# A decoder layer on one Trainium2 core: the gate product in rounded parts, and the last 32 columns of the projection in four column groups

## The chip, the cores and the metric

The kernel runs on one core of a Trainium2 chip. The metric is the device time of one execution in microseconds. Engines are named as in the profile: PE is TensorE's matmul, PEld its weight load, DVE is VectorE, ACT is ScalarE, POOL is GpSimd, and SP is SyncE, which here issues most of the DMAs. Each engine works through its own instructions strictly in the order in which the program gives them to it; an instruction that waits holds up all that stand behind it on the same engine.

## What is computed

One decoder layer on x of (1, 256, 1024) float32. Cut to what matters here:

```
z = rms_norm(x, norm1_g) @ w_in                 # 1024 -> 1824 (RWKV) + 1536 (MoBA) + 2048 (gates)
z[:, :1824] is mixed with its row before: z + mu * (shift_right(z) - z)
r, k, v = three blocks of 512 columns           # columns 0 .. 1535
xw, xa, xg = z[..., 1536:1600], z[..., 1600:1664], z[..., 1664:1824]   # 64, 64 and 160 columns
decay = exp(-exp(w_log)),  w_log from decay_bias + tanh(xw) @ w_decay_up
a = sigmoid(aaa_bias + xa @ w_aaa_up)
g = sigmoid(xg) @ w_gate_up                     # 160 -> 512: "the gate product"
y = delta-rule recurrence over 256 steps, 8 heads of 64, then a group norm
rwkv = (y + bonus(r, k, v)) * g
moba = softmax attention of 8 heads on q, k, v of the MoBA columns
out = x + merge(rwkv, moba) @ w_out, then a gated MLP with a causal convolution (1024 -> 2 x 2816 -> 1024)
```

## The kernel before

**Weights in two parts.** Nearly all of the PE's work is products of the large weight matrices with 256 tokens. A float32 weight tile of 128x1024 numbers (512 KB) comes from memory through SP's queue (`load_next`, L241), in the order of one list, `queue` (L329 ff.). ACT rounds it to fp32r into `whi` (L253, `split_hi`), DVE subtracts that from the original into `wlo` (L263, `split_lo`), and the PE forms three products: `whi` with the input's high part, `whi` with its low part, `wlo` with its high part. In the functions `wst` (L291, L293, L296) the weight is stationary, and 24 matmuls of 128x256 use up one tile; in `xst` (L312, L313, L316) the input is stationary and the weights stream by. Few buffers stand between these steps (4 for raw tiles, 4 further ones for the first loads, 4 of `whi`, 3 of `wlo`, 3 PSUM banks under the name `acc`), so that each engine runs only a tile or two ahead of the PE.

**Small products in float32.** The two low-rank products of decay and a (L549), the gate product (L787, L788), the sums over heads (L585, L786) and the recurrence use float32 matmuls directly, which the trace records as two matmul passes each.

**The first steps.** Transposes of the normalised input, the first two weight tiles (columns 1536 to 1791: xw, xa and the first 128 columns of xg) and the filler matmuls of `keep_warm` (L374: five matmuls of 128x512 on a tile of ones, between the transposes of the two token halves) are written in a fixed order for all engines. `shift` (L354 on ACT, L355 on DVE) mixes a projected block with its row before. The remaining 32 columns of xg are made from a third weight tile, the tail: columns 1696 to 1823, 128 of them, of which 96 are there already. Its loads are pieces of 512 bytes, its 24 matmuls are the ones of `run(wst(p, 1, hh, hl))`, and its result goes to `xg[:, 1]`. The weight rows that would count a column twice are zero in `wgu[:, 1]`.

**What sets the order after that.** Two threads written as Python generators, "chain" (L543 ff., the RWKV recurrence) and "bulk" (L1122 ff., projections k, r, MoBA's q, v, and so on), are interleaved by a small planner (L1152 ff.). A thread yields a cost (the PE time that it has just issued) and a latency (how long until it can go on), and the planner picks the next thread by these estimates. The order on PE follows from it; a scheduler then sets the order on ACT, DVE, POOL and SP from its own model of the program.

**The chain** around the change: the products of decay and a (`at`, `ch`, L549), eight sigmoids on ACT (`sg`, `av`, L554), a scan over tokens on DVE (L561), then exponentials on ACT. The mixed k is squared on ACT (`sq`, L579) and summed over heads on PE (`pss`, L585). Later the chunk matrices `G` are made (L660), moved by DMA through a scratch `d` into `Tb` (L670, L672), inverted on DVE (`tmp`, `mid`, `Xb`, L697 to L728), moved through `d` again into `X` (L740), and used by the PE in 64 matmuls of 32x32, `pp` (L814). Between the `G` and the `pp` of the PE's order stand weight products of bulk and the block `bon`: bonus sums (L786) and gate product (L787, L788) in two halves of 12 passes, with a yield of 2.7 after each half.

In the diff `b2`, `b4`, `b8`, `t1`, `by` and `cst.tile` hand out buffers of different pools, `atp()`, `chp()` and `acc()` hand out PSUM banks.

Of the kernel before, what the change touches and what calls it, by code (L numbers as in the profile page):

```python
# [9 lines left out]
F32 = mybir.dt.float32  # L10
# [8 lines left out]
S = 256  # L19
# [3 lines left out]
CW = 512  # L23
# [13 lines left out]
def body(tc, x, positions, norm1_g, w_in, rwkv_mu, w_decay_up, decay_bias, w_aaa_up,  # L37
# [5 lines left out]
    with ctx:  # L43
# [59 lines left out]
        ones = cst.tile([128, 512], mybir.dt.bfloat16, name="ones")  # L103
# [10 lines left out]
        rst = cst.tile([128, 4 * S], mybir.dt.bfloat16, name="rst")  # L114

        def late_consts():
            pool.memset(rst, 1.0)
            pool.memset(rst.rearrange("p (c i) -> p c i", i=64)[:, :, 0:1], 0.0)
            pool.memset(wgu[0:96, 1], 0.0)
# [39 lines left out]
        wgu = cst.tile([128, 2, CW], F32, name="wgu")  # L159
# [4 lines left out]
        for r, n in ((mu1[0:1792].rearrange("(n c) -> n c", c=128), 14),  # L164
                     (mu1[1696:1824].rearrange("(n c) -> n c", c=128), 1),
# [4 lines left out]
        loads += [(wdu[0:64], w_decay_up[0]), (wdu[64:128], w_aaa_up[0]),  # L170

                  (wgu[:, 0], w_gate_up[0, 0:128]), (wgu[96:128, 1], w_gate_up[0, 128:160])]
# [156 lines left out]
        queue += kh(win, 1536, 256) + kh(win, 1696, 128)  # L329
# [27 lines left out]

        def first_steps():
# [23 lines left out]
            nc.gpsimd.dma_start(*loads.pop(4))  # L382
# [8 lines left out]
            for t in range(2):  # L391
# [23 lines left out]
                if t == 0:  # L415
                    keep_warm(5)
# [55 lines left out]
            late_consts()  # L472
            xwa = t1("xwa")
            xg = b2("xg", [128, 2, S])
            shift(xwa, p[:, 0:256], 12)
            act.activation(xwa[0:64], xwa[0:64], AF.Tanh)
            shift(xg[:, 0], p[:, 256:512], 13)
            split_lo()
            split_hi()
            return xwa, xg  # L480

        E = mybir.EngineType
        with tc.manual_schedule(engines={E.PE, E.Activation, E.DVE, E.Pool}):
            xwa, xg = first_steps()
# [14 lines left out]
        p = acc()  # L499
        run(wst(p, 1, hh, hl))  # L500
        shift(xg[:, 1], p[:, 0:256], 14)
# [41 lines left out]
        def chain():  # L543

            sg, av, kp = b4("sg"), b4("av"), b4("kp")
            pw = [[(chp if j else atp)() for _ in range(2)] for j in range(2)]
            for ct in range(4):
                for n, lo_ in enumerate((0, 64)):
                    pe.matmul(pw[ct // 2][n][:, ct % 2 * 256:ct % 2 * 256 + 256],  # L549
                              wdu[lo_:lo_ + 64, ct * 128:(ct + 1) * 128],  # L550
                              xwa[lo_:lo_ + 64], start=True, stop=True)
            for ct in range(4):
# [3 lines left out]
            yield 2.2, 3.0  # L556
            act.activation(xg[:, 0], xg[:, 0], AF.Sigmoid)
            act.activation(xg[:, 1], xg[:, 1], AF.Sigmoid)
# [221 lines left out]
            A1 = b4("A1")  # L780
            for j in range(2):
                p, pg = (chp(), chp("pg")) if j else (atp(), atp("pg"))
                for i in range(2):
# [3 lines left out]
                    pe.matmul(pg[:, os], wgu[:, 0, cs], xg[:, 0], start=True, stop=False)  # L787
# [563 lines left out]
```

## Time and profile before

| | before |
|---|---|
| median of 3 runs | 412.95 us (411.76 to 413.96) |
| the profiled execution's own time | 411.65 us |
| its span in the trace | 409.5 us |
| PE busy | 402.8 us, 98% of the span |
| ACT, DVE busy | 234.1 us (57%), 317.9 us (78%) |
| POOL busy | 35.1 us (9%) |
| memory read | 68.76 MB, 171 GB/s over the span |

The span is the stretch from the first to the last instruction of the profiled execution; 2.15 us of its time lie around it. Matmuls overlap one another in the pipeline, so what one costs is read from the distance between two starts and not from its duration.

### The profile page before, as it was taken

Reading aid. Unit: us, or ns where it says so; the run is one execution under the profiler, and the core shown is the slowest. Engines: PE = TensorE matmul, PEld = TensorE weight load, DVE = VectorE, ACT = ScalarE, POOL = GpSimd, SP = SyncE. Lnnn points to the kernel's source line nnn. Section 1 sums busy time; section 2 is a strip of 40 time slices with the busy share of each in tenths; the row PEclk is TensorE's granted clock in tenths of the full one; section 3 lists DMA queues with packets and bytes.
Section 4 is the critical chain, followed back from the end, with each engine's and each line's share of the span. In section 5 each row is a group of like instructions: output and inputs, shape, how many; then the busy total and the mean of one; then the engine's idle time right before and its main releaser. Section 6 shows DMA issues by size and latency. Waiting matters only on the chain.

```text
span 409.5 us, 8251 instructions
## 1 busy us (share of the span) xinstructions
PE 402.8 (98%) x3266; PEld 352.6 (86%) x3266; DVE 317.9 (78%) x535; ACT 234.1 (57%) x393; POOL 35.1 (9%) x67
## 2 busy tenths in 40 slices
PE   8999999999999999999999999999999999999996
PEld 4999898898899889999988888888888888888885
DVE  3878999769547886677975898968769678697694
ACT  6999576254567774443554864635545555465450
POOL 8600410123100010000000000000000000000000
PEclk9999999999999999999999999999999999999999
DMA  8964556642953153366565557566655656656612
GB/s 256 317 216 120 172 174 173 196 125 72 232 163 106 53 154 106 107 205 205 189 204 175 156 158 228 179 205 186 210 176 173 209 185 199 202 168 203 196 54 102
DMA packets 60042, 70.72 MB, mean 173 GB/s; under 512 B 6530, under 2 KB 50325, under 8 KB 60005
## 3 DMA queue, kind: packets, MB, share of 16 engines
q1 hardware_dynamic: 59078, 69.79, 56.9%
q0 software_dynamic: 880, 0.41, 0.6%
q8 instruction: 25, 0.41, 0.4%
q14 instruction: 13, 0.10, 0.1%
q10 hardware_dynamic: 46, 0.01, 0.0%
HBM read 68.76 MB, written 1.44 MB: 171 GB/s over the span
## 4 chain that ended last, share of the span: by engine, by line
PE 85%; DVE 8%; DMA 3%; issue 1%; ACT 1%; POOL 1%; POOLq 0%; DVEq 0%; ACTq 0%
PE acc L1232 20%; PE acc L1237 10%; PE acc L291 7%; PE acc L293 7%; PE acc L296 7%; PE f L1252 4%; PE f L1254 4%; PE f L1256 4%; PE acc L312 4%; PE acc L313 3%; PE acc L316 3%; DVE wlo L263 2%; PE idle L452 1%; PE idle L374 1%; DMA X<-d 1%
## 5 line engine op out<-in xcount | busy, mean ns | idle before, releaser
L253 ACT CAST whi<-raw 128x1024 fp32r<-128x1024 f32 x123 | 128.7, 1051 | 106.7 <-PE acc L1232 41.0
L263 DVE TENSOR_TENSOR wlo<-raw,whi 128x1024 fp32r<-128x1024 f32 x123 | 150.7, 1229 | 42.8 <-PE acc L1237 14.0
L1232 PE MATMUL acc<-hx,whi 128*128 128x512 f32 x352 | 89.5, 395 | 0.0
L1232 PEld LDWEIGHTS acc<-hx,whi 128*128 128x128 f32 x352 | 63.4, 188 | 12.4
L291 PE MATMUL acc<-hx,whi 128*128 128x256 f32 x232 | 58.9, 289 | 0.6 <-DVE qkv L989 0.6
L293 PE MATMUL acc<-hx,whi 128*128 128x256 f32 x232 | 56.7, 280 | 0.0
L1237 PEld LDWEIGHTS acc<-hx,wlo 128*128 128x128 f32 x352 | 46.8, 188 | 4.0
L1237 PE MATMUL acc<-hx,wlo 128*128 128x256 f32 x352 | 47.4, 277 | 0.0
L291 PEld LDWEIGHTS acc<-hx,whi 128*128 128x128 f32 x232 | 43.8, 189 | 2.8 <-issue 2.1
L293 PEld LDWEIGHTS acc<-hx,whi 128*128 128x128 f32 x232 | 43.8, 189 | 0.1
L296 PE MATMUL acc<-hx,wlo 128*128 128x256 f32 x232 | 36.2, 279 | 0.0
L1254 PE MATMUL f<-whi,hb 128*128 128x512 f32 x80 | 31.2, 390 | 0.0
L1256 PE MATMUL f<-wlo,hb 128*128 128x512 f32 x80 | 31.2, 390 | 0.0
L1252 PE MATMUL f<-whi,hb 128*128 128x512 f32 x80 | 31.2, 389 | 0.0
L296 PEld LDWEIGHTS acc<-hx,wlo 128*128 128x128 f32 x232 | 31.0, 189 | 0.0
L1242 DVE TENSOR_REDUCE an<-acc 128x256 f32<-128x512 f32 x22 | 14.2, 686 | 9.4 <-PE acc L1237 9.4
L312 PE MATMUL acc<-whi,hx 128*128 128x512 f32 x48 | 19.8, 413 | 0.0
L313 PE MATMUL acc<-whi,hx 128*128 128x512 f32 x48 | 18.8, 393 | 0.0
L1256 PEld LDWEIGHTS f<-wlo,hb 128*128 128x128 f32 x80 | 15.0, 188 | 3.2
L1252 PEld LDWEIGHTS f<-whi,hb 128*128 128x128 f32 x80 | 15.0, 188 | 2.8
L1254 PEld LDWEIGHTS f<-whi,hb 128*128 128x128 f32 x80 | 15.0, 188 | 2.8
L316 PE MATMUL acc<-wlo,hx 128*128 128x512 f32 x48 | 14.9, 392 | 0.0
(319 smaller groups left out, 616.5 us busy)
## 6 DMA issues: line engine op xcount, KB each, us to landing
raw<-in_w_ffn_up_dram SPq DMA_DIRECT2D x44, 512.0 KB, 4.1
raw<-in_w_in_dram SPq DMA_DIRECT2D x42, 512.0 KB, 4.7
raw<-in_w_ffn_down_dram SPq DMA_DIRECT2D x22, 512.0 KB, 4.1
raw<-in_w_out_dram SPq DMA_DIRECT2D x8, 512.0 KB, 4.3
x<-in_x_dram SPq DMA_DIRECT2D x8, 256.0 KB, 3.4
raw<-in_w_branch_b_dram SPq DMA_DIRECT2D x4, 512.0 KB, 3.4
raw<-in_w_branch_a_dram SPq DMA_DIRECT2D x4, 512.0 KB, 4.6
out_dram<-o SPq DMA_DIRECT2D x3, 256.0 KB, 2.1
```

The costliest lines, as they stand in the source:

```text
L253: act.copy(hi[:, :k * c], raw[:, :k * c])
L263: eng.tensor_tensor(lo[:, :n], raw[:, :n], hi[:, :n].bitcast(F32), op=OP.subtract)
L291: pe.matmul(om, wh[:, k, ms], xh[:, k0 + k], start=k0 + k + m == 0, stop=False, skip_group_check=True)
L293: pe.matmul(om, wh[:, k, ms], xl[:, k0 + k], start=False, stop=False, skip_group_check=True)
L296: pe.matmul(om, wl[:, k, ms], xh[:, k0 + k], start=False, stop=k0 + k == nk - 1 and m == n - 1, skip_group_check=True)
L312: pe.matmul(ps_[t], xh[:, K, ts], wh[:, k], start=K == 0, stop=False)
L313: pe.matmul(ps_[t], xl[:, K, ts], wh[:, k], start=False, stop=False)
L1232: pe.matmul(ps_[m], wh[:, k, m * 128:m * 128 + 128], hx[:, k0 + k].rearrange("p a s -> p (a s)"), start=k0 + k == 0, stop=False, skip_grou ...
L1237: pe.matmul(ps_[m][:, 0:S], wl[:, k, m * 128:m * 128 + 128], hh[:, k0 + k], start=False, stop=k0 + k == 7, skip_group_check=True)
L1252: pe.matmul(fin[f], hb[:, 0, i, ts], wh[:, 0, cs], start=st, stop=False, skip_group_check=f == 3)
L1254: pe.matmul(fin[f], hb[:, 1, i, ts], wh[:, 0, cs], start=False, stop=False, skip_group_check=f == 3)
L1256: pe.matmul(fin[f], hb[:, 0, i, ts], wl[:, 0, cs], start=False, stop=False, skip_group_check=f == 3)
```

## The change

1. The tail tile, its 24 matmuls, its split into parts and its shift go. A tile `wtr` of 8x32 columns (128 KB, in pieces of 128 bytes) is loaded by SP third, behind the second raw tile. Sixteen float32 matmuls with 32 columns each (L488 of the changed file) go into four groups of 32 PSUM partitions, group g taking the k-blocks g and g + 4. DVE copies the result (`tls`), and one float32 matmul with a constant `fold3` (L584) adds the four groups and repeats the sum three times over 96 partitions, where it is shifted into `xgt` (L589, L590). POOL makes `fold3` with four small copies.
2. The gate product's inputs and weights are split into fp32r parts: `wgh` and `wgl`, `xgp` in two parts, and on 96 partitions `wgt` and `xtp`, which hold all three products of the 32 columns. `gate_parts` makes them with four casts on ACT and four subtractions on DVE; its weights `wgr` are loaded by SP behind the projection of k. The eight float32 matmuls become sixteen fp32r matmuls of 256 columns.
3. Both halves of `bon` are issued in one run, with one yield of 2.8.
4. `keep_warm(5)` becomes `keep_warm(3)`.
5. The second PSUM bank of MoBA's query product comes from `chp` instead of `acc`.
6. The first stage of `pp` and `P` is 16 columns wide instead of 32.
7. Yields: the chain begins with 0, 1.0, and its first cost is 2.6; in the group norm the latencies before the transposes `pc` are 7.0, 5.5, 5.5 and 0.8 for the four chunks, where they were 5.5, 5.5, 5.5 and 2.8. The attention's query and key pieces wait for the chain's turn (`joined`).
8. `ones` and `rst` live in other buffers, and the row of mu for the 32 columns is loaded four times.

The diff, cut to its core:

```diff
-        queue += kh(win, 1536, 256) + kh(win, 1696, 128)
+        queue += kh(win, 1536, 256)
...
                 load_next(i == 0, early=i >= NRAW)
+                if i == 1:
+                    nc.sync.dma_start(wtr, win[:, :, 1792:1824])
...
-                    keep_warm(5)
+                    keep_warm(3)
...
+            tl = chp("tl")[:, 0:S]
+            for n, xx in enumerate((hh, hl)):
+                for k in range(8):
+                    g = k % 4
+                    pe.matmul(tl[32 * g:32 * g + 32], wtr[:, k], xx[:, k].bitcast(F32), start=n == 0 and k < 4,
+                              stop=n == 1 and k >= 4, skip_group_check=True)
...
+            dve.tensor_copy(tls, tl)
...
-        p = acc()
-        run(wst(p, 1, hh, hl))
-        shift(xg[:, 1], p[:, 0:256], 14)
...
+        def gate_parts():
+
+            for w, o in wgr:
+                act.copy(o, w)
+            dve.tensor_tensor(wgl, wgr[0][0], wgh.bitcast(F32), op=OP.subtract)
+            dve.tensor_tensor(wgt[64:96], wgr[1][0][64:96], wgt[64:96].bitcast(F32), op=OP.subtract)
+            act.copy(xgp[:, 0], xg)
+            act.copy(xtp[0:96], xgt[0:96])
+            dve.tensor_tensor(xgp[:, 1], xg, xgp[:, 0].bitcast(F32), op=OP.subtract)
+            dve.tensor_tensor(xtp[32:64], xgt[32:64], xtp[32:64].bitcast(F32), op=OP.subtract)
...
+            yield 0, 1.0
...
+            pf = chp("fold")[0:96, 0:S]
+            pe.matmul(pf, fold3, tls, start=True, stop=True)
...
+            act.activation(xgt[0:96], pf, AF.Copy, scale=omm[0:96, 14:15])
+            dve.scalar_tensor_tensor(xgt[0:96, 1:S], pf[:, 0:S - 1], par[0:96, MU + 14:MU + 15], xgt[0:96, 1:S],
+                                     op0=OP.mult, op1=OP.add)
-            yield 2.2, 3.0
+            yield 2.6, 3.0
...
-                    pe.matmul(pg[:, os], wgu[:, 0, cs], xg[:, 0], start=True, stop=False)
-                    pe.matmul(pg[:, os], wgu[:, 1, cs], xg[:, 1], start=False, stop=True)
-                yield 2.7, 0.2
+                    pe.matmul(pg[:, os], wgh[:, cs], xgp[:, 0], start=True, stop=False)
+                    pe.matmul(pg[:, os], wgh[:, cs], xgp[:, 1], start=False, stop=False)
+                    pe.matmul(pg[:, os], wgl[:, cs], xgp[:, 0], start=False, stop=False)
+                    pe.matmul(pg[:, os], wgt[:, cs], xtp[0:96], start=False, stop=True)
+            yield 2.8, 0.2
...
-            pp = two_banks("pp", 32)
+            pp = two_banks("pp", 16)
...
-                    yield 0, 5.5 if c < 3 else 2.8
+                    yield 0, (7.0, 5.5, 5.5, 0.8)[c]
...
             yield from proj4("k", 4)
-            for _ in range(4):
+            wgr.append((b2("wgr", [128, CW]), wgh))
+            wgr.append((b2("wgr", [96, CW]), wgt))
+            nc.sync.dma_start(wgr[0][0], w_gate_up[0, 0:128])
+            for r in range(3):
+                nc.sync.dma_start(wgr[1][0][32 * r:32 * r + 32], w_gate_up[0, 128:160])
+            for _ in range(2):
                 nc.sync.dma_start(*loads.pop(0))
...
-                ps_ = [acc(), acc()]
+                ps_ = [acc(), acc() if i else chp("acc")]
...
             yield from attention_input(0)
+            gate_parts()
```

The line numbers of the changed file are some 7 to 40 higher than those of before. The order of instructions moves at three places.

On ACT, in the first steps, before: the casts of the tiles k1, k2 and k3 (the second to fourth tile of the projection of k), and the eight sigmoids.

```order
L253 CAST whi<-raw 128x1024 [waits DMAHW6_49,Pool_49]
L253 CAST whi<-raw 128x1024 [waits DMAHW7_49,Pool_49]
L354 ACTIVATE xg<-acc,omm 128x256 [waits PE_49]
L253 CAST whi<-raw 128x1024 [waits DMAHW0_49]
L554 ACTIVATE sg<-at,par 128x256 [waits PE_49]
L554 ACTIVATE av<-at,par 128x256 [waits PE_49]
```

The same place on ACT after the change; the two casts are k2 and k3.

```order
L260 CAST whi<-raw 128x1024 [waits DMAHW7_49,Pool_49]
L260 CAST whi<-raw 128x1024 [waits DMAHW0_49,Pool_49]
L593 ACTIVATE xg<-xg 128x256 [waits DVE_49]
L525 CAST wgh<-wgr 128x512 [waits DMAHW5_49]
L587 ACTIVATE sg<-at,par 128x256 [waits PE_49]
L587 ACTIVATE av<-at,par 128x256 [waits PE_49]
```

The cast of the gate's weights, although `gate_parts` stands late in the code, is ordered ahead of the eight sigmoids; it waits for the load of `wgr`, which SP issues behind the last tile of the projection of r.

On DVE, before: the low part of k2, the scan behind the sigmoids, and the low parts of k3 and r0. The rows left out are small operations of the rotary tables.

```order
L263 TENSOR_TENSOR wlo<-raw,whi 128x1024 [waits DMAHW7_49,DVE_49,PE_49]
...
L561 SCALAR_TENSOR_TENSOR L<-rst,sg 128x1024 [waits Activation_49,Pool_49]
L205 TENSOR_SCALAR turns<-turns 128x32 [waits DVE_49]
L211 SCALAR_TENSOR_TENSOR ang<-turns,ang 128x32 [waits DVE_49] x3
L263 TENSOR_TENSOR wlo<-raw,whi 128x1024 [waits DMAHW0_49,PE_49]
```

And after:

```order
L270 TENSOR_TENSOR wlo<-raw,whi 128x1024 [waits DMAHW7_49,Activation_49,Pool_49]
L526 TENSOR_TENSOR wgl<-wgr,wgh 128x512 [waits DMAHW5_49,Activation_49]
L597 SCALAR_TENSOR_TENSOR L<-rst,sg 128x1024 [waits Activation_49,Pool_49]
L590 SCALAR_TENSOR_TENSOR xgt<-fold,par,xgt 96x255 [waits Activation_49]
L270 TENSOR_TENSOR wlo<-raw,whi 128x1024 [waits DMAHW0_49,DVE_49,PE_49]
```

The subtraction of the gate's weights now stands between the low parts of k2 and k3, and the low part of k3 still stands behind the scan.

On PE, around `bon`, before: the second half of `bon` with a run of six projection matmuls ahead of it (one of six such runs between the first half and `pp`).

```order
L788 MATMUL pg<-xg,wgu 128x256
L312 MATMUL acc<-whi,hx 128x512
L313 MATMUL acc<-whi,hx 128x512
L312 MATMUL acc<-whi,hx 128x512
L313 MATMUL acc<-whi,hx 128x512
L316 MATMUL acc<-wlo,hx 128x512 x2
L786 MATMUL ch<-zr,bones 128x256
L787 MATMUL pg<-xg,wgu 128x256
L788 MATMUL pg<-xg,wgu 128x256
```

And after, the join of the two halves:

```order
L827 MATMUL pg<-xtp,wgt 128x256
L823 MATMUL ch<-zr,bones 128x256
L824 MATMUL pg<-xgp,wgh 128x256
L825 MATMUL pg<-xgp,wgh 128x256
L826 MATMUL pg<-xgp,wgl 128x256
L827 MATMUL pg<-xtp,wgt 128x256
```

The run of six is gone from between the halves. Five runs of six stand between `bon` and `pp` in both, so that 36 projection matmuls between the first half and `pp` have become 30; one run of six has moved behind the second half of `pp`. The rows of the chain from `G` to `X` on DVE, POOL and SP stand in the same order in both.

More of the change, by code (lines that the diff above doesn't have):

```diff
@@ L102, in body @@
         AR = b8("AR", [128, 16, 2, 64])
-        ones = cst.tile([128, 512], mybir.dt.bfloat16, name="ones")
+        ones = b2("ones", [128, 512], mybir.dt.bfloat16)
         jp = t1("jp", (128, 128), I32)
@@ L113, in body @@
         spread16 = cst.tile([128, 128], F32, name="spread16")
-        rst = cst.tile([128, 4 * S], mybir.dt.bfloat16, name="rst")
+        rst = b2("rst", [128, 4 * S], mybir.dt.bfloat16)
+        fold3 = cst.tile([128, 96], F32, name="fold3")
         def late_consts():
+            for g in range(4):
+                gs = slice(32 * g, 32 * g + 32)
+                pool.tensor_copy(fold3[gs].rearrange("p (r i) -> p r i", r=3),
+                                 ident[gs, gs][:, None, :].to_broadcast([32, 3, 32]))
             pool.memset(rst, 1.0)
             pool.memset(rst.rearrange("p (c i) -> p c i", i=64)[:, :, 0:1], 0.0)
-            pool.memset(wgu[0:96, 1], 0.0)
             pool.memset(bones, 0.0)
@@ L158, in body @@
         wdu = cst.tile([128, CW], F32, name="wdu")
-        wgu = cst.tile([128, 2, CW], F32, name="wgu")
+        wgh = cst.tile([128, CW], F32R, name="wgh")
+        wgl = cst.tile([128, CW], F32R, name="wgl")
+        wgt = cst.tile([96, CW], F32R, name="wgt")
         gqk = cst.tile([128, 2, 64], F32, name="gqk")
@@ L169, in body @@
             at_ += n
-        loads += [(wdu[0:64], w_decay_up[0]), (wdu[64:128], w_aaa_up[0]),
-                  (wgu[:, 0], w_gate_up[0, 0:128]), (wgu[96:128, 1], w_gate_up[0, 128:160])]
+            if at_ == 14:
+                loads.append((p1[14:15].rearrange("o (g c) -> o g c", g=4),
+                              bass.AP(tensor=mu1.tensor, offset=mu1.offset + 1792, ap=[[0, 1], [0, 4], [1, 32]])))
+                at_ += 1
+        loads += [(wdu[0:64], w_decay_up[0]), (wdu[64:128], w_aaa_up[0])]
         for i, g in enumerate((q_norm_g, k_norm_g)):
@@ L356, in shift @@
                                                   op0=OP.mult, op1=OP.add).ins)
+        wtr = b2("wtr", [128, 8, 32])
         def first_steps():
@@ L780, in chain @@
             A1 = b4("A1")
+            bp_ = [(chp(), chp("pg")) if j else (atp(), atp("pg")) for j in range(2)]
             for j in range(2):
-                p, pg = (chp(), chp("pg")) if j else (atp(), atp("pg"))
+                p, pg = bp_[j]
                 for i in range(2):
@@ L786, in chain @@
                     pe.matmul(p[:, os], bones, bp[:, ct], start=True, stop=True)
-                    pe.matmul(pg[:, os], wgu[:, 0, cs], xg[:, 0], start=True, stop=False)
-                    pe.matmul(pg[:, os], wgu[:, 1, cs], xg[:, 1], start=False, stop=True)
-                yield 2.7, 0.2
+                    pe.matmul(pg[:, os], wgh[:, cs], xgp[:, 0], start=True, stop=False)
[3 more added lines that the diff above has]
+            yield 2.8, 0.2
+            for j in range(2):
+                p, pg = bp_[j]
                 dve.tensor_tensor(bon[:, 2 * j:2 * j + 2].rearrange("p a b -> p (a b)"), p,
@@ L841, in chain @@
                         s_ = quad(1 - a, h)
-                        pe.matmul(pt[s_.start:s_.start + 16, u], P[s_, u // 8, u % 8, 0:16],
+                        pe.matmul(pt[s_.start:s_.start + 16, u], P[s_, u // 8, u % 8],
                                   X[s_, u, 32 * h + 16:32 * h + 32], start=True, stop=True)
@@ L974, in body @@
         ybs = []
+        wgr = []
         def finish_qk(p, i, t):
@@ L1015, in attention @@
                     yield 0.4, 1.0
+                    while not joined[0] and "chain" not in done:
+                        yield 0, 0.1
                 qkT.append(dT)
```

25 lines of the change are left out of this document (14 added, 11 removed).

## The prediction

> **What bounds the kernel now.** First I read the shares of the span, the slices and the chain that ended last, then PE's waits, then the stages that the diff touches.
>
> ```profile
> span 409.5 us, 8251 instructions
> PE 402.8 (98%) x3266; PEld 352.6 (86%) x3266; DVE 317.9 (78%) x535; ACT 234.1 (57%) x393; POOL 35.1 (9%) x67
> ...
> PE   8999999999999999999999999999999999999996
> ...
> PEclk9999999999999999999999999999999999999999
> ...
> PE 85%; DVE 8%; DMA 3%; issue 1%; ACT 1%; POOL 1%; POOLq 0%; DVEq 0%; ACTq 0%
> ```
>
> The first line is the page's, then busy shares, two of the rows in 40 slices, and the chain by engine. PE's list of waits:
>
> ```profile
> PE idle L374 <- DVE eps L369: 1.5, 1, 1.5
> PE pS L941 <- DVE VU L935: 0.6, 1, 0.6
> PE acc L291 <- DVE qkv L989: 0.6, 1, 0.6
> PE pc L900 <- DVE yc L894: 0.4, 1, 0.4
> PE pp L814 <- DMA X<-d: 0.2, 1, 0.2
> ```
>
> PE is the bound, at full clock, from the second slice to the last but one. Behind the start it waits some 2 us in all. So two things decide: how many PE passes go, and whether the other engines still deliver when PE arrives earlier or they later. The span is 409.5 us, the profiled execution took 411.65, and that is 1.3 below the median of 412.95. I sum against 411.65 and apply the difference to the median.
>
> **The 32 columns, filler and fold.**
>
> ```profile
> 7.59 1.24 PE L374 MATMUL idle<-ones 128*128 128x512 bf16 x5
> 8.67 1.04 PE L413 MATMUL xt<-ident,xn 128*128 128x128 f32 x8
> ...
> 15.57 0.28 PE L291 MATMUL acc<-hx,whi 128*128 128x256 f32 x1
> 17.38 1.07 PE L296 MATMUL acc<-hx,wlo 128*128 128x256 f32 x8
> 18.38 1.13 PE L549 MATMUL at<-xwa,wdu 64*128 64x256 f32 x8
> ...
> 38.88 0.67 PE L585 MATMUL pss<-sq,bones 128*32 128x256 f32 x8
> 39.48 0.38 PE L291 MATMUL acc<-hx,whi 128*128 128x256 f32 x1
> ...
> 95.82 0.60 PE L786 MATMUL ch<-zr,bones 128*128 128x256 f32 x2
> 96.25 0.59 PE L787 MATMUL pg<-xg,wgu 128*128 128x256 f32 x2
> ```
>
> The tail's 24 matmuls run from 15.57 to 18.38: 2.81 us go. In their place stand 16 float32 matmuls in four column groups, 32 passes. The nearest row is `pss`, which is the same form: four float32 matmuls, 8 passes, one per group, from 38.88 to 39.48, that is 0.60. Four times that is 2.4; with the switch into and out of the narrow form paid once instead of four times (the row behind `pss` is 0.38 long where the usual one is 0.28, so 0.1 each), I take 2.1. If the groups did not overlap, 32 passes would go at the step of full-width float32, 0.43 for two (95.82 to 96.25), and be 6.9; `pss` speaks against that, since its 8 passes would be 1.7. The `fold` is two more passes, +0.43. Two filler matmuls less are 2 x 0.22 = −0.43 (five of them hold PE from 7.59 to the transposes at 8.67), or nothing if PE then waits for its input instead. Sum: −2.81 + 2.1 + 0.43 − 0.43 = **−0.7**.
>
> **The cast that now stands ahead of the sigmoids** is the largest term.
>
> ```profile
> 18.04 2.55 SPq L1126 DMA_DIRECT2D wgu<-in_w_gate_up_dram  x2
> ...
> wgu<-in_w_gate_up_dram SPq DMA_DIRECT2D x1, 256.0 KB, 8.8
> ...
> 15.57:18.38 2.81, 2.81 (x26) 2.68 (x25) 1.60 (x4) 2.11 (x5) 2.56 (x9) 1.00 1.10 348
> ```
>
> These are the issue of the gate's weights on SP's queue, the size and time to landing of the larger load, and a window whose last number is GB/s. The timelines of ACT and of DVE:
>
> ```profile
> 19.73 1.03 ACT L253 CAST whi<-raw 128x1024 fp32r<-128x1024 f32 x1
> 20.67 0.47 ACT L554 ACTIVATE sg<-at,par 128x256 f32<-128x256 f32 x1
> 23.18 0.48 ACT L554 ACTIVATE av<-ch,par 128x256 f32<-128x256 f32 x1
> 24.64 1.06 ACT L253 CAST whi<-raw 128x1024 fp32r<-128x1024 f32 x1
> 30.76 1.03 ACT L253 CAST whi<-raw 128x1024 fp32r<-128x1024 f32 x1
> 37.09 0.50 ACT L579 ACTIVATE sq<-zk,par 128x256 f32<-128x256 f32 x1
> ```
>
> ```profile
> 23.40 2.29 DVE L561 TENSOR_TENSOR_SCAN L<-rst,sg 128x1024 f32<-128x1024 bf16 x1 [0.29 <-ACT sg L554]
> 26.36 1.22 DVE L263 TENSOR_TENSOR wlo<-raw,whi 128x1024 fp32r<-128x1024 f32 x1
> ```
>
> The gate's weights were issued at 18.04 and landed 8.8 later, at 26.84, behind four weight tiles in a full stream (348 GB/s). After the change they have the same place in SP's order, behind r3. Ahead of them 512 KB of tail are gone and 128 KB of `wtr` have come: at 348 GB/s, 1.5 us less and 0.4 more, so they land at about 25.7. If the 1024 small pieces took the time of the tail's 1024 larger ones, nothing would be saved and it would be 26.8; without `wtr`, 25.3. Before, nothing waited for this load until the gate product at 92 us. Now ACT's cast of `wgh` waits for it, and behind that cast stand the eight sigmoids, which before began at 20.67; on DVE the subtraction of `wgl` waits with it, and behind it the scan and the low part of k3.
>
> Worked forward on ACT: the cast ends at 25.7 + 0.6 = 26.3 (half the size of one of 1.05, and a start). The eight sigmoids take 20.67 to 23.53, so 2.9: 29.2. From there to the end of the cast of r1 the old rows have 23.53 to 31.79, 8.3, and a little more for the narrow shift: 37.7. From that cast to the last square (37.09 + 0.50) they have 5.8: 43.5, so `pss`, which was at 38.88, starts at about 43.6.
>
> On DVE the scan needs the last `sg`, the sixth sigmoid, so it starts at 26.3 + 6 x 0.36 = 28.5 or a little later, ends at 30.8, and the low part of k3 follows the narrow shift (0.5) and takes 1.2: ready at about 32.5. Before, it was ready at 26.36 + 1.22 = 27.58. PE wants it after k0, k1, k2 and eight matmuls of k3. In the old order the last `ch` ended about 20.3 (18.38 + two runs of 0.97), and three tiles of 2.81 and 8 x 0.117 make 29.7; with the change it is some 0.5 to 0.7 earlier: 29.2. So PE stands for 3.2 us there, then for about 0.9 at r1's high part (37.7 against 34.36 − 0.7 + 3.2 = 36.9), and for 1.3 at `pss`. The sum, stalls of 5.4 less 0.7 of work, is the same 4.7 that ACT's chain gives: **+4.7**, with −0.7 inside it. Landing and sum go one for one: with 26.8 it is +5.8, and nothing but the −0.7 is left only where the weights land 5.4 sooner, at about 20.3, when the sigmoids used to begin.
>
> By the Trainium skill ("DMA: Bandwidth & Descriptors", Specifications) transfers under 512 bytes miss the line rate, since the engine reads, modifies and writes; `wtr` has pieces of 128 bytes. By that the weights land near the upper of my two ends, and the sum is some 1 us higher; no row here has pieces of that size in a full queue.
>
> **The second bank** of the query product no longer waits for `qkv`: −0.6 (the row of PE's waits), and nothing is late in its place, as the scheduler's order has no new wait there.
>
> **Gate product and `pp`.**
>
> ```profile
> L787 PE MATMUL pg<-xg,wgu x8: 379/379/379, 92.3 to 97.8; 128*128 128x256 f32 x8
> ...
> 94.00 0.59 PE L788 MATMUL pg<-xg,wgu 128*128 128x256 f32 x2
> 94.24 0.58 PE L312 MATMUL acc<-whi,hx 128*128 128x512 f32 x1
> ```
>
> The gate's group and two rows of PE's timeline; then the chain that ended last, between `G` and `pp`:
>
> ```profile
> 77.96 1.81 DVE G L660 x3
> ...
> 80.65 2.49 DMA d<-G
> ...
> 84.65 3.60 DMA Tb<-d
> ...
> 97.26 1.71 DMA d<-Xb
> ...
> 100.70 4.98 DMA X<-d
> 105.77 0.73 PE pp L814 x47
> ```
>
> L787 and L788 have 8 passes each, at 0.43 for two: 3.45 us. The 16 new matmuls are of the fp32r form of L291, which goes at 2.81 / 24 = 0.117: 1.9. So PE has **−1.6** less to do. The joined run also moves six projection matmuls (94.24 to 95.82 with a switch, 1.4 without) behind `pp`. The four pieces at 96 partitions may cost a switch in and out, 8 x 0.1.
>
> But the chain shows what PE waits for at `pp`: `G` at 77.96, then two trips through memory and the inversion on DVE, and `X` in place at 105.7. Its rows keep their order, so it still takes 27.8 us from `G` to `pp`. PE had filled that stretch to within 0.2. With 1.6 + 1.4 = 3.0 less work in it, PE now stands **+3.0** longer at `pp`. The gate's saving is used up there, and the six matmuls moved behind cost their 1.4 later. If the switches cost their 0.8, they fill idle time and change nothing. Four casts and four subtractions more (ACT 57%, DVE 78% busy) lie beside PE's work, except for the first pair above. Sixteen columns instead of 32 in `pp` I take as 0: the 62 passes of 32x32 take 0.65 us, some 10 ns each, so little of it can be streaming; at most −0.3.
>
> **The later waits.** `pS` 0.6 and `pc` 0.4 are what the new latencies of the group norm (0.8 for the last chunk) and `joined` can remove, and joined small runs save a switch or two of 0.1. I take −1.2 with the switches. At most −1.2; at worst each wait comes back at another row, 0.
>
> **The sum.** −0.7 + 5.4 − 0.6 − 1.6 + 3.0 − 1.2 = **+4.3**: 411.65 becomes 415.9, and the median 412.95 becomes 417.2.
>
> **The rivals.**
>
> *The early wait is covered (no change).* If ACT's cast does not hold back the sigmoids (the weights land by 20.3, or ACT and DVE catch up in gaps between their rows), the term of 5.4 is gone: 4.3 − 5.4 = −1.1, 411.9. For it: ACT is busy 57% over the whole. Against it: the load's own row, 8.8 us behind a full queue, and the rows above, which hardly have gaps in this stretch.
>
> *Neither wait bites (faster).* If `X` comes sooner too, because the chain's transfers or DVE's part of it (78% busy) have slack that shows once PE runs ahead, the 3.0 goes as well: −4.1, 408.9. Against it: the chain from 77.96 to 105.77 is unbroken.
>
> *The change does not do what it says*: the gate's parts save PE passes and no time. That is in the forecast already; it decides by `X`'s landing alone, and without it my sum would be 414.2.
>
> *The column groups run one behind the other (slower still).* 6.9 instead of 2.1 is +4.8, of which the stall of 3.2 at k3 absorbs most: +1.6, 418.8. It decides where less than two groups overlap. For slower at all the one mechanism is the early cast: its price passes the savings once the weights land after 25.7 − 4.3 = 21.4.
>
> *The clock falls.* In the rows of before PEclk is 9 throughout and the longest idle stretch in the middle is 0.6 us; the stalls of 3.2 and 3.0 would be the first of their kind. If the granted clock were halved behind each for as long as the stall lasted, half of 3.2 and of 3.0 would come late: 420.3. By the Trainium skill ("TensorE: Matmul & The Clock Gate", Part 1) one idle window of about 3.4 us halves the clock; no row here shows a stall so long.
>
> **How the numbers follow.** Forecast, early cast and `pp` wait both: 0.58, between 414.5 and 419. Covered early wait: 0.17. Neither: 0.13. Serial groups or a fallen clock: 0.12. Half a per cent, 2.1 us, is about what a measurement of this kernel tells from no change. Faster takes the "neither" case and the lower edge of the covered one: 0.18. Same takes the rest of that and the forecast's lower edge, with 412.95 ± 2.1: 0.22. Slower: 0.60. The range reaches from 409.5, in the middle of the faster case, to 420.5, with the fallen clock.
>
> **What would show it.** Right: an idle stretch of 5 to 7 us on ACT that ends with the cast of `wgh` at about 26, PE waiting for `wlo` about 3 us near 29, `pss` near 43.6, and an idle stretch of about 3 us before `pp`, released by the DMA into `X`. Sixteen narrow matmuls in about 2.1 us. Wrong: sigmoids at about 21 as before, or the weights in place by 20; or `pp` starting less than 27 us behind `G`. The waits of `pS`, `pc` and `qkv` should be gone from PE's list.

## The result, and the profile after

| | before | after |
|---|---|---|
| median (6 runs each) | 412.57 us (411.76 to 413.96) | 416.96 us (414.89 to 418.71) |
| ratio of the runs, 95% interval | 1 | 1.0103 [1.0069, 1.0137] |
| profiled execution, span | 411.65 us, 409.5 us | 416.85 us, 415.1 us |

The change makes the kernel 1.0% slower, 4.4 us. The forecast was 417.2 us. The page of the kernel after, its first lines, PE's two rows in 40 slices and the chain by engine:

```profile
span 415.1 us, 8282 instructions
...
PE 403.3 (97%) x3274; PEld 351.3 (85%) x3274; DVE 317.4 (76%) x539; ACT 234.1 (56%) x396; POOL 42.1 (10%) x70
...
PE   7989998999799999999999999999999999999996
...
PEclk9998999999899999999999999999999999999999
...
PE 70%; DVE 14%; DMA 6%; ACT 5%; issue 2%; POOL 1%; SPq 1%; DVEq 0%; POOLq 0%; ACTq 0%
```

PE's busy time has not fallen, although matmul work went: 403.3 us after 402.8. Work at a slower clock counts as busy for longer, and PEclk is 8 in two slices, the fourth and the eleventh. PE's list of waits, and the one of ACT's that is new:

```profile
PE acc L303 <- DVE wlo L270: 3.3, 2, 2.0
PE pp L855 <- DMA X<-d: 2.1, 2, 1.6
PE idle L385 <- DVE eps L380: 1.5, 1, 1.5
PE xt L424 <- DVE xn L417: 0.9, 2, 0.6
PE pc L941 <- DVE Sn L990: 0.4, 1, 0.4
...
ACT wgh L525 <- DMA wgr<-in_w_gate_up_dram: 5.2, 1, 5.2
```

The waits of `pS` and of `qkv` are gone, `pc` is there still, and two waits for `wlo` and a longer one for `X` have come. The timelines of SP, ACT and DVE, and of PE (start, duration, and in brackets the idle time ahead of an instruction):

```profile
16.06 1.23 SPq L1171 DMA_DIRECT2D wgr<-in_w_gate_up_dram  x1
```

```profile
19.09 0.42 ACT L593 ACTIVATE xg<-xg 128x256 f32<-128x256 f32 x1
24.68 0.62 ACT L525 CAST wgh<-wgr 128x512 fp32r<-128x512 f32 x1 [5.18 <-DMA wgr<-in_w_gate_up_dram]
25.20 0.47 ACT L587 ACTIVATE sg<-at,par 128x256 f32<-128x256 f32 x1
```

```profile
27.60 2.29 DVE L597 TENSOR_TENSOR_SCAN L<-rst,sg 128x1024 f32<-128x1024 bf16 x1 [1.58 <-ACT sg L587]
...
30.18 2.35 DVE L270 TENSOR_TENSOR wlo<-raw,whi 128x1024 fp32r<-128x1024 f32 x2
```

```profile
15.38 1.93 PE L488 MATMUL tl<-hx,wtr 128*32 128x256 f32 x32
17.25 0.39 PE L298 MATMUL acc<-hx,whi 128*128 128x256 f32 x1
...
29.19 0.28 PE L300 MATMUL acc<-hx,whi 128*128 128x256 f32 x1
31.45 0.74 PE L303 MATMUL acc<-hx,wlo 128*128 128x256 f32 x4 [1.98 <-DVE wlo L270]
32.02 0.28 PE L298 MATMUL acc<-hx,whi 128*128 128x256 f32 x1
32.14 0.38 PE L300 MATMUL acc<-hx,whi 128*128 128x256 f32 x1
...
33.38 0.41 PE L300 MATMUL acc<-hx,whi 128*128 128x256 f32 x1
33.59 1.05 PE L303 MATMUL acc<-hx,wlo 128*128 128x256 f32 x4
...
41.88 1.14 PE L621 MATMUL pss<-sq,bones 128*32 128x256 f32 x8
42.96 0.38 PE L298 MATMUL acc<-hx,whi 128*128 128x256 f32 x1
```

The weights, issued at 16.06, are there at 24.66 (the chain gives their load as 8.60). ACT stands from 19.5 to 24.68, the sigmoids begin at 25.20 instead of 20.67, the scan follows at 27.60, and the low part of k3 is ready at 31.39. PE stands for it for 2.0 us. Behind that a matmul of 128x256 takes 0.41 instead of 0.28, at steps of 0.21 instead of 0.115, for 3.4 us. In windows of the same execution (third number from the end the granted clock) this reads:

```profile
30.00:32.00 2.00, 0.55 (x4) 0.56 (x5) 2.00 (x3) 1.70 (x2) 0.00 (x0) 1.00 0.00 0
32.00:34.00 2.00, 2.00 (x12) 2.00 (x11) 0.71 (x2) 1.99 (x4) 0.00 (x0) 0.54 0.03 8
34.00:36.00 2.00, 2.00 (x13) 2.00 (x12) 0.12 (x1) 2.00 (x5) 0.00 (x0) 0.60 0.00 0
36.00:38.00 2.00, 2.00 (x20) 2.00 (x19) 1.73 (x12) 2.00 (x4) 0.00 (x0) 1.00 0.02 4
...
110.00:112.00 2.00, 2.00 (x8) 1.57 (x7) 0.16 (x1) 0.00 (x0) 0.00 (x0) 0.67 1.05 370
112.00:114.00 2.00, 2.00 (x6) 1.29 (x4) 1.06 (x1) 0.00 (x0) 0.00 (x0) 0.50 1.03 348
```

The second fall of the clock lies behind the wait at `pp`. PE's timeline there:

```profile
106.07 0.62 PE L323 MATMUL acc<-wlo,hx 128*128 128x512 f32 x2
108.30 0.20 PE L855 MATMUL pp<-X,G 32*32 32x16 f32 x2 [1.61 <-DMA X<-d]
109.02 0.70 PE L855 MATMUL pp<-X,G 32*32 32x16 f32 x62 [0.52 <-DMA X<-d]
...
111.54 0.63 PE L319 MATMUL acc<-whi,hx 128*128 128x512 f32 x1
111.97 0.63 PE L320 MATMUL acc<-whi,hx 128*128 128x512 f32 x1
```

A matmul of 128x512 takes 0.63 at steps of 0.43 instead of 0.39 at 0.23. So behind each of the two waits of some 2 us the matmuls take about 1.6 us longer than at full clock. Whether that is lost time is another question: behind `pp` it is, at k3 it is not (the filler run below).

By stages, from the starts of PE's instructions in the two profiled executions, this is where the 5.6 us between the spans come from:

| stage | before ends | after ends | measured | predicted |
|---|---|---|---|---|
| start to the end of `pss` | 39.48 | 42.96 | +3.5 | +4.7 |
| to the end of the last `G` on DVE | 80.35 | 84.74 | +0.9 | −0.6 |
| to the second half of `pp` | 109.39 | 114.19 | +0.4 | 0 (−1.6 + 3.0 − 1.4) |
| to the end | 409.46 | 415.06 | +0.8 | +0.2 (+1.4 − 1.2) |

The profiled execution of before lies 0.9 us below its median, which is most of why the spans differ by more than the medians. Between `G` and `pp` the chain of the changed kernel reads:

```profile
82.35 1.81 DVE G L696 x3
...
85.04 3.37 DMA d<-G
...
89.71 2.50 DMA Tb<-d
...
101.28 1.71 DMA d<-Xb
...
104.71 4.17 DMA X<-d
109.02 0.70 PE pp L855 x51
```

From that row of `G` to the bulk of `pp` it takes 26.7 us, where it took 27.8 (77.96 to 105.77). DVE's part, from the first `Xb` to the transfer of `Xb`, is as long as before (8.98 and 8.92 us); the transfers are not: 3.37 us for 2.49, 2.50 for 3.60, 4.17 for 4.98, together 1.0 us less. Why they are shorter is not shown. The +0.4 of the third row is thus 1.6 us of the slow clock less 1.1 us by which `X` comes sooner behind `G`.

### The profile page after: what moved, and what is told of

It is laid out like the page before. It is cut to its first block, busy times and chain, and to the rows that moved or that the text cites. A ratio compares the mean times of both kernels' runs of the same rounds, so it can differ in the third digit from the quotient of the medians.

```text
span 415.1 us, 8282 instructions
## 1 busy us (share of the span) xinstructions
PE 403.3 (97%) x3274; PEld 351.3 (85%) x3274; DVE 317.4 (76%) x539; ACT 234.1 (56%) x396; POOL 42.1 (10%) x70
## 4 chain that ended last, share of the span: by engine, by line
PE 70%; DVE 14%; DMA 6%; ACT 5%; issue 2%; POOL 1%; SPq 1%; DVEq 0%; POOLq 0%; ACTq 0%
PE acc L1282 20%; PE acc L1287 10%; PE f L1304 4%; PE f L1302 4%; PE f L1306 4%; PE acc L298 4%; PE acc L303 4%; PE acc L300 4%; DVE wlo L270 4%; PE acc L319 3%; PE acc L323 3%; PE acc L320 3%; DMA wgr<-in_w_gate_up_dram 2%; ACT sc L1090 1%; DMA X<-d 1%
## 5 line engine op out<-in xcount | busy, mean ns | idle before, releaser
L1282 PEld LDWEIGHTS acc<-hx,whi 128*128 128x128 f32 x352 | 63.4, 188 | 12.4
L298 PE MATMUL acc<-hx,whi 128*128 128x256 f32 x224 | 57.8, 292 | 0.0
L300 PE MATMUL acc<-hx,whi 128*128 128x256 f32 x224 | 55.4, 282 | 0.0
L1287 PE MATMUL acc<-hx,wlo 128*128 128x256 f32 x352 | 47.3, 277 | 0.0
L298 PEld LDWEIGHTS acc<-hx,whi 128*128 128x128 f32 x224 | 43.0, 192 | 2.3 <-issue 1.0
L300 PEld LDWEIGHTS acc<-hx,whi 128*128 128x128 f32 x224 | 43.0, 192 | 0.2
L303 PE MATMUL acc<-hx,wlo 128*128 128x256 f32 x224 | 35.4, 281 | 3.3 <-DVE wlo L270 3.3
L319 PE MATMUL acc<-whi,hx 128*128 128x512 f32 x48 | 19.9, 415 | 0.0
L323 PE MATMUL acc<-wlo,hx 128*128 128x512 f32 x48 | 15.8, 413 | 0.1
```

The lines of the kernel that those rows point to most:

```text
L298: pe.matmul(om, wh[:, k, ms], xh[:, k0 + k], start=k0 + k + m == 0, stop=False, skip_group_check=True)
L300: pe.matmul(om, wh[:, k, ms], xl[:, k0 + k], start=False, stop=False, skip_group_check=True)
L303: pe.matmul(om, wl[:, k, ms], xh[:, k0 + k], start=False, stop=k0 + k == nk - 1 and m == n - 1, skip_group_check=True)
L319: pe.matmul(ps_[t], xh[:, K, ts], wh[:, k], start=K == 0, stop=False)
L1282: pe.matmul(ps_[m], wh[:, k, m * 128:m * 128 + 128], hx[:, k0 + k].rearrange("p a s -> p (a s)"), start=k0 + k == 0, stop=False, skip_grou ...
L1287: pe.matmul(ps_[m][:, 0:S], wl[:, k, m * 128:m * 128 + 128], hh[:, k0 + k], start=False, stop=k0 + k == 7, skip_group_check=True)
```

## The experiments

The kernel before was run beside each group of kernels, with medians of 411.96, 412.46 and 412.71 us, so ratios to it are compared; 0.0024 are 1 us. The changed kernel stands at 1.0103.

**The cast put late.**

```diff
-            gate_parts()
+            with tc.issue_after(last_exp[1]):
+                gate_parts()
```

> The parts of the gate's weights are made only after the square root behind the sums over heads (about 43 us), nothing else is changed. Theory 1 (the early cast is the main cost: 2.0 us of waiting at the low part of k3, 1.6 us by the halved clock behind it, 0.5 us in the sums): the sigmoids begin near 21 us again, no PE wait near 29 us, clock 1.00 there, the sums near 38.4 us, and 417.0 - 4.1 = 412.9 us. Rival (the loss sits at the later wait for X, and PE would wait there for what it gains early): within 1 us of 417.0, with a longer wait at pp.

418.38 us, ratio 1.0150 [1.0128, 1.0172]: no faster, rather slower. The sigmoids do begin at 21.56, right behind the products, and from those products to `pss` it takes 19.9 us instead of 23.0. But the products begin 1.5 us later in this execution (20.39), so that the sums end only 1.2 us sooner. The rest came back at other places, and the scheduler moved more than the cast: 11 of the first 16 matmuls of the block `pgr` (that makes `G`) now stand 40 weight matmuls earlier in PE's order, and PE waits there. Two rows of its waits:

```profile
PE pp L855 <- DMA X<-d: 2.1, 2, 1.7
...
PE pgr L692 <- ACT KBt L684: 1.4, 1, 1.4
```

From the sums to the last `G` it takes 1.5 us longer than in the changed kernel, and from there to the second half of `pp` 1.6 us longer: the clock stays at half for 6.8 us behind the wait. So this run tells nothing of the cast's price; for that every order has to stay as it is.

**The bonus and gate block in two halves.**

```diff
-            bp_ = [(chp(), chp("pg")) if j else (atp(), atp("pg")) for j in range(2)]
...
                     pe.matmul(pg[:, os], wgt[:, cs], xtp[0:96], start=False, stop=True)
-            yield 2.8, 0.2
-            for j in range(2):
-                p, pg = bp_[j]
+                yield 1.4, 0.2
```

> The bonus and gate block is issued in two halves again, so that six projection matmuls stand between them and 36 ahead of pp, as before the change. Theory 2 (PE waits at pp because X comes at a fixed distance behind G and PE has less to do): the wait at pp falls from 2.1 to about 0.7 us, pp starts at the same time, the six matmuls come off the time behind it: 417.0 - 1.4 = 415.6 us, and 414.0 us if the shorter wait also keeps the clock up. Rival (X itself comes later when the halves are apart, or the order there does not matter): 417 us, wait at pp as long as in the changed kernel.

414.21 us, 1.0047 [1.0032, 1.0063], 2.3 us less than the change. PE's wait at `pp` is 0.8 us, `pp` starts 0.6 us sooner, and the clock is 1.00 behind it: the second half of `pp` follows 3.58 us behind the first, as before (3.62) and not 5.17. From there to the end it takes 299.4 us instead of 300.9, which is the price of the six matmuls. So theory 2 holds by the stages, with the clock. The totals do not separate the two: the one run of the changed kernel at a mean clock of 1.000 took 414.89 us, 1.0056 of the median beside it, and the three of this kernel at 1.000 took 1.0052 to 1.0062.

**Filler ahead of `pp`.** 

```diff
+            fl = atp("fill")
+            for _ in range(14):
+                pe.matmul(fl[:, 0:256], hh[:, 0, 0:128], hh[:, 0], start=True, stop=True)
             pp = two_banks("pp", 16)
```

> Fourteen matmuls of 128x256 without use (1.6 us) stand ahead of pp, on data that is there; nothing else is changed, the result is not touched. Theory 3 (a PE wait of some 2 us lets the clock fall, and that costs about 1.6 us at half clock behind pp): with the filler the granted clock stays at 1.00 behind pp, and the time is 417.0 - 1.6 = 415.4 us against those runs in which the clock fell. Rival (the clock has nothing to do with the idle stretch, or the filler only delays pp): 417.0 us or up to 1.6 us more, with the clock falling as before.

415.18 us (415.11 to 415.56), 1.0077 [1.0060, 1.0094]. The filler's 14 matmuls fill the wait, `pp` starts at the same time, and the windows behind it hold the clock:

```profile
108.00:110.00 2.00, 1.48 (x69) 1.20 (x68) 1.21 (x2) 0.27 (x1) 0.00 (x0) 1.00 0.81 108
110.00:112.00 2.00, 2.00 (x11) 1.62 (x10) 0.67 (x1) 0.36 (x1) 0.00 (x0) 1.00 1.08 376
112.00:114.00 2.00, 2.00 (x71) 1.48 (x69) 0.84 (x2) 1.50 (x3) 0.00 (x0) 1.00 1.10 333
```

From the first to the second half of `pp` it takes 3.59 us instead of 5.17: the fall of the clock costs 1.6 us, and work without use takes it away. The total moved by 1.1 us in ratio, with intervals that overlap; the clock did not fall in every run of the changed kernel (below).

This run also prices the other fall. In its profiled execution the clock still falls behind a wait of 2.1 us for k3 (mean clock 0.996), in the three others it stays up (0.999 to 1.000), and all four take 415.11 to 415.56 us: the fall at k3 costs nothing that the total shows. From the first sigmoid to the end of the sums it takes 17.75 us here (25.00 to 42.76) and 17.75 in the changed kernel (25.20 to 42.96), both with the slow clock in between, and 17.75 in the two halves, where PE waited 1.4 us for k3 and the clock stayed up:

```profile
24.73 0.47 ACT L587 ACTIVATE sg<-at,par 128x256 f32<-128x256 f32 x1
...
42.48 0.39 PE L298 MATMUL acc<-hx,whi 128*128 128x256 f32 x1
```

There PE, at full clock, waits 0.6 us for a high part and 0.9 within the sums instead, both times for ACT. So with the late sigmoids it is ACT's chain that sets when the sums end, and not PE's clock.

**The gate in float32.** The gate product takes the loaded weights directly, `gate_parts` and its eight instructions go.

```diff
-                    pe.matmul(pg[:, os], wgh[:, cs], xgp[:, 0], start=True, stop=False)
-                    pe.matmul(pg[:, os], wgh[:, cs], xgp[:, 1], start=False, stop=False)
-                    pe.matmul(pg[:, os], wgl[:, cs], xgp[:, 0], start=False, stop=False)
-                    pe.matmul(pg[:, os], wgt[:, cs], xtp[0:96], start=False, stop=True)
+                    pe.matmul(pg[:, os], wgr[0][0][:, cs], xg, start=True, stop=False)
+                    pe.matmul(pg[:, os], wgr[1][0][0:32, cs], xgt[0:32], start=False, stop=True)
...
-            gate_parts()
```

> The gate product is taken in float32 as before the change (8 matmuls, 16 passes, from the loaded weights and 32 partitions of the narrow part); no casts, no subtractions, all else of the change stays. Theories 1 to 3 together: no early cast (-4.1), no subtractions on DVE (the PE wait of 1.5 us for a low part near 70 us goes), 1.6 us more PE work that only fills the wait at pp, clock up behind it: 417.0 - 4.1 - 1.5 = 411.4 us, or 409.8 us with the clock held at pp. Rival (the gate's fewer passes are a real saving): 417.0 - 4.1 + 1.6 = 414.5 us.

413.82 us (413.59 to 413.89), 1.0041 [1.0026, 1.0056]: between the two expectations. No PE wait for a low part near 29, none at `pp`, clock 1.00. But a wait for a low part, which the changed kernel has at 70.65 us, is there still (at 66.08), without any subtraction on DVE:

```profile
PE acc L303 <- DVE wlo L270: 1.2, 1, 1.2
```

So that wait, 1.3 us in the changed kernel, is not caused by the added subtractions alone. Without either of the two waits this kernel is still 1.7 us slower than the one before: its sums end 1.4 us later (40.87 for 39.48) and the last `G` another 1.2. Why is not shown.

**The load put early.** The 256 KB of `wgr` are issued ahead of r0. The orders on PE, ACT, DVE and POOL are the same as in the changed kernel; ties to earlier instructions (`gi`, `on`, `mixed[1]`) hold them there.

```diff
+                if i == 5:
+                    nc.sync.dma_start(wgr0, w_gate_up[0, 0:128])
...
-            wgr.append((b2("wgr", [128, CW]), wgh))
-            wgr.append((b2("wgr", [96, CW]), wgt))
-            nc.sync.dma_start(wgr[0][0], w_gate_up[0, 0:128])
+            wgr.extend([(wgr0, wgh), (b2("wgr", [96, CW]), wgt)])
...
+            with tc.issue_after(gi[0]), tc.issue_after(mixed[1]):
+                gate_parts()
```

> Only the load of the gate's larger weight piece (256 KB) moves: it is issued ahead of r0 instead of behind r3; every engine keeps its instructions and their order, the cast included (one reduction on DVE is held to its place). Theory 1 (ACT stands for 5.2 us behind that load; the sigmoids, the scan and the low part of k3 behind it stop PE for 2.0 us, and 1.6 us follow at half clock): the cast runs near 19.5 us, the low part of k3 is in time, from the products of decay and a to the sums over heads it takes 20 us instead of 23.0, and 417.0 - 3.1 = 413.9 us. Rival (the chain behind it gives the time back, as it did when the cast was put late): 416 us or more.

412.36 us (10 runs, 410.31 to 414.22), 1.0000 [0.9975, 1.0025]: 4.2 us less than the change in ratio, more than expected. The cast runs as soon as ACT is free:

```profile
19.81 0.41 ACT L598 ACTIVATE xg<-xg 128x256 f32<-128x256 f32 x1
20.12 0.60 ACT L530 CAST wgh<-wgr 128x512 fp32r<-128x512 f32 x1
20.71 0.47 ACT L592 ACTIVATE sg<-at,par 128x256 f32<-128x256 f32 x1
```

From the products to `pss` it takes 18.9 us instead of 23.0. One load in another place of a queue was worth the whole loss. The wait at `pp` is still there (2.4 us), and the clock falls behind it: 0.50 in the windows from 106 to 110 us, and low for 6.8 us in all (104.7 to 111.5).

**Early load and two halves.** Both edits above.

> Early load and two halves of the bonus and gate block together. If the two costs are separate (theories 1 and 2): the 414.2 us of the two halves less the 2.1 us that its early stretch was still longer, 412.1 us, no PE wait for a low part near 29 us, at most 0.8 us at pp, clock 1.00 throughout. Rival (one wait takes the place of the other): 414.2 us.

409.33 us (409.15 to 409.39), 0.9932 [0.9911, 0.9953]: faster than before, by 0.7%, and 2.8 us below 412.1. Nothing but the wait at the start, for `xn`, 0.8 us at `pp` and 0.6 at `pc` is left in PE's list, and all runs have a clock of 0.999 or 1.000. The two costs are separate, and taking away both gave more than their sum as I had set it: the wait near 70 us is gone too. It was 0.8 us (at 66.16) with the early load alone, and why it went is not shown.

**The second bank.** 

```diff
-                ps_ = [acc(), acc() if i else chp("acc")]
+                ps_ = [acc(), acc()]
```

> The second PSUM bank of MoBA's query product comes from the old place again; all engines keep their order. Theory of the prediction (the change saves the 0.6 us wait for that bank): 417.0 + 0.6 = 417.6 us, with the wait for qkv back. Rival (DVE is full between 45 and 73 us, so PE waits there for one thing or the other): 417.0 us within 0.3, the wait for a low part near 70 us (1.5 us) shorter by the 0.6 us that come back at the bank.

418.03 us, 1.0150 [1.0124, 1.0176]. It is on the side of the prediction's term and larger: PE now waits near 68 us for a high part on ACT, and the clock falls there (0.64 in the window from 70 to 74 us).

```profile
PE acc L298 <- ACT whi L260: 3.0, 2, 2.4
```

In ratio that is 1.9 us above the changed kernel, with intervals that overlap at their ends (1.0124 and 1.0137). The rival, that PE waits there for one thing or the other at the same cost, finds no support; the size stays uncertain.

**The small parts on POOL.** Early load, two halves, and

```diff
-            dve.tensor_tensor(wgt[64:96], wgr[1][0][64:96], wgt[64:96].bitcast(F32), op=OP.subtract)
+            pool.tensor_tensor(wgt[64:96], wgr[1][0][64:96], wgt[64:96].bitcast(F32), op=OP.subtract)
```

with the same for the two subtractions of `xgp` and `xtp`.

> As early load and two halves, and the three smaller subtractions of the gate's parts (1.5 us of DVE near 64 us) are made by POOL instead. Theory 4 (in the stretch from 45 to 73 us DVE is the bound, so each of its instructions there is PE's time): the wait of 1.4 us for a low part near 70 us goes and the time is some 1.4 us below the early load with two halves, 410.7 us, which would be below the kernel before. Rival (the wait there comes from the order of the low parts, not from the added instructions, as it also stood at 1.2 us with the gate in float32): within 0.4 us of the early load with two halves.

408.39 us (408.17 to 408.98), 0.9913 [0.9894, 0.9931], the fastest of all. The wait near 70 us that was to go was not there any more. What is left of the gain, 0.9 us, comes with `G`: from the end of the sums to the end of its last piece on DVE it takes 39.6 us (38.89 to 78.51) instead of 40.6 (39.35 to 79.96), and 39.6 again in the run with five fillers below. The intervals of this kernel and the one before it overlap, so the gain over 409.33 is likely and not shown.

**Float32 in two halves.** The gate in float32 and the two halves, the load in the changed kernel's place, where nothing waits for it early.

> The gate product in float32 (no parts, no casts) with the bonus and gate block in two halves, the rest of the change as it is. It prices the parts themselves once neither wait is in the way. Theory 2 (X comes at its own time, PE had at most 0.8 us of slack at pp with the parts, so 1.6 us more gate work costs 0.8 us, and DVE and ACT are free of eight instructions): 409.33 + 0.8 = 410.1 us, at most 0.2 us of PE wait at pp. Rival (the saved passes are worth their full 1.6 us): 410.9 us or more. Rival (the parts cost more on DVE and ACT than they save): 409 us or less.

413.94 us (413.25 to 415.0), 1.0028 [1.0011, 1.0046], the same as the float32 gate in one run (1.0041 [1.0026, 1.0056]). That is the counterpart of theory 2: where PE comes to `pp` late, as it does with the longer gate, the place of the six matmuls is worth nothing. Against early load and two halves it is 4.0 us slower in ratio, and not 0.8: the scheduler's order on DVE differs too, and PE waits 1.3 us for a low part near 66 us. From the block's start to `pp` it takes 15.1 us instead of 13.4, so 1.7 us of the difference lie in the gate itself.

**Five fillers.** The fastest kernel with `keep_warm(5)`.

> The fastest kernel so far (early load, two halves, small parts on POOL; 408.39 us) with five filler matmuls instead of three. Theory 5 (the two fillers saved nothing, since PE waits for the normalised input in their place): 408.4 us within 0.3, the wait for xn gone from PE's list. Rival of the prediction's sum (each filler is 0.22 us of PE time): 408.8 us. Third possibility (fewer fillers let the clock start lower in some runs): 408.0 us with less scatter.

409.21 us, 0.9916 [0.9902, 0.9931], against 0.9913 with three: no difference. The wait for `xn` did not go (1.3 us in this profiled execution, 0.2 in that of three fillers).

## Why the prediction was right, and where its steps were off

The time came as forecast, and by the two mechanisms that the forecast named. **The early cast**: ACT's idle stretch was to be 5 to 7 us, ending near 26 with the cast of `wgh`; it was 5.2, ending at 24.68. PE was to wait about 3 us for the low part of k3; it was 2.0. With the load moved and every order kept, 4.2 us go. **The wait at `pp`**: 3.0 were expected; 2.1 were there, and two halves took away 2.3 us of the total, the clock's part included. The rival "neither wait bites" was 4.1 us below the kernel before; the kernel with early load and two halves, where 0.8 us of the wait at `pp` are left, is 2.8 us below it. What decided was put rightly: a load that nobody had waited for, and a chain through memory with its own length.

But the sizes inside the sum were off, and the errors largely cancelled: by the stages above they are −1.2, +1.5, +0.4 and +0.6 us. That the median came within 0.3 us of the forecast is luck. One of the prediction's own signs of being wrong came true: `pp` came less than 27 us behind `G`, 26.7 by the rows of the two chains.

- *The landing of the weights*, 25.7 us: measured 24.66, 1.0 sooner than that and sooner than the lower bound of 25.3. The load was issued 2.0 us sooner than before (16.06 for 18.04) and landed 8.6 us later instead of 8.8. I had taken the stream of before, 348 GB/s. In the window from 15 to 17 us it was 385 in the changed kernel; why is not settled. By the Trainium skill ("DMA: Bandwidth & Descriptors", Specifications) the pieces of 128 bytes should have made the load later than my middle value; the landing shows none of that. The trace's packets do show a price by the byte: 13 ns for a piece of 128 bytes, 49 ns for one of 1024 at that time. But 1024 pieces of 13 ns over 16 engines are 0.8 us, where I had set 0.4 for their bytes, too little to show.
- *The stalls*, 5.4 us: 3.2 were set at k3, 0.9 at r1 and 1.3 at `pss`. There were 2.0 at k3, none at r1 and 0.5 inside `pss`. The low part was ready 1.1 sooner, as the weights were. The later two came to less because PE, at half clock, arrived 1.6 us later by itself. The other working of the same term, by ACT's chain, was the better one: sigmoids 4.5 us later than before (25.20), the sums at 41.88 instead of 43.6.
- *The clock*, which I had as a rival of its own within 0.12: it fell behind both stalls, 2.0 and 2.1 us long, where I had asked for 3.2 and 3.0. At k3 the fall cost nothing, since the sums waited for ACT (17.75 us with and without it). Behind `pp` it cost 1.6 us, and there it belonged into the sum.
- *The second bank*, −0.6: the step said that nothing is late in its place. In the stretch to `G` the changed kernel lost 0.9 us instead, with the wait of 1.3 us for a low part at 70.65. With the bank taken back the kernel is rather slower still, so the step's sign seems right. That the late sigmoids push work into a stretch where DVE has few gaps would explain the wait (0.8 us with the load early, none with the two halves as well), but it stood at 1.2 us with the gate in float32, whose sigmoids are not late, so its cause stays open.
- *The gate's passes*, −1.6: the block with the sums takes 3.63 us (95.67 to 99.30) where its two halves took 4.80, so −1.2. The turn from the float32 sums to the fp32r gate costs an extra step each time, 0.31 instead of 0.12 between the first two gate matmuls, in PE's timeline after:

```profile
95.91 0.47 PE L824 MATMUL pg<-xgp,wgh 128*128 128x256 f32 x1
96.22 0.28 PE L825 MATMUL pg<-xgp,wgh 128*128 128x256 f32 x1
96.34 0.28 PE L826 MATMUL pg<-xgp,wgl 128*128 128x256 f32 x1
```

- *`X` at a fixed distance from `G`*, 27.8 us: it took 26.7, or 24.3 instead of 25.4 counted from the end of `G`, and between 24.1 and 24.9 in every other run with the gate in parts. The rows kept their order, as I had said, but the transfers between them did not keep their length. That is why the wait was 2.1 and not 3.2.
- *The 32 columns*: 2.1 us were set, `tl` takes 1.87 (15.38 to 17.25). The groups overlap; the rival that they don't falls. The `fold` took 0.32 to the next start. The fillers, −0.43, saved nothing, the other end given for them.
- *The later waits*, −1.2: `pS` went, `pc` stayed at 0.4. From `px` to the transposes of the MLP's parameters the kernel with early load and two halves is 0.3 us shorter than before (74.9 against 75.2), the one with two halves alone 0.6 (74.7), so about −0.3 to −0.6.
- *`pp` with 16 columns*, 0: 62 passes in 0.63 us after, 0.65 before.

## What to carry to other kernels

Look for what an added instruction waits for and what stands behind it on its engine: a cast that costs 0.6 us held eight sigmoids for 5 us because its load stood last in a full queue, and moving that load, with nothing else, gave back all of it. Work removed ahead of a wait that has its own length is not time removed; put other work there, or leave what was there. But a chain that keeps its order need not keep its length, as the transfers between `G` and `pp` show, and a slow clock costs time only where PE is what the next step waits for. When an experiment moves an instruction in a scheduled program, compare the orders on all engines first, or it measures the scheduler.

## What the runs showed of the hardware

A PE wait of about 2 us in full work can halve the clock for about 3.4 us, so that its matmuls take 1.6 us longer; in the late cast and the early load it stayed low for 6.8 us, and from the first to the second half of `pp` it took 6.39 us there. By the Trainium skill ("TensorE: Matmul & The Clock Gate", Part 1) one idle window of about 3.4 us throttles the clock, and the window runs freely. The slow stretch in the changed kernel is as long as one such window (32.1 to 35.5 us), and 6.8 us is as long as two; the idle time needed here was less, 1.98 and 1.61 + 0.52 us. That it depends on where the wait falls fits with the runs: the mean clock of one execution was anything from 0.991 to 1.000 with the same program. In the ten runs of the early load, where the one long wait left behind the start is that at `pp`, the time went with it:

| mean granted clock | time, us |
|---|---|
| 0.999 and 1.000 | 410.31, 410.90 |
| 0.994 to 0.995 | 411.47, 411.77, 412.22, 412.51, 413.01 |
| 0.991 | 413.52, 413.92, 414.22 |

In the changed kernel the run at 1.000 took 414.89 us and the three at 0.991 took 416.85 to 418.71, so part of its scatter of 3.8 us is likely the clock's. Not all scatter is: runs of the kernel before lay between 411.4 and 414.5 us at a mean clock of 0.998 and more, and what moved them stays open. A PE wait of 1.4 us (two halves alone, near 31 us) left the clock at 1.00 behind it, and so did the one of 1.3 us at 70.65 in the changed kernel. In the run of the second bank so did longer ones, 1.78 us at k3 and 1.56 + 0.55 at `pp`, about as long as those that halved it elsewhere; the one of 2.41 us near 68 halved it.
